# Router logits computed with the 36 logits as rows of PSUM, one table of places, expert weights computed later, and the first expert pair's tokens turned alone

## The chip, the cores and the metric

The kernel runs on one NeuronCore of one Trainium2 chip. The metric is the device time of one execution in microseconds (us). TensorE (PE in the profile, PEld for its weight loads) multiplies into PSUM; VectorE (DVE), ScalarE (ACT) and GpSimd (POOL) do the rest; SyncE (SP) issues the loads of weights, and POOL issues the DMAs that gather token rows. TensorE's clock is granted at one of two levels, 1.2 and 2.4 GHz; the profile prints it as 0.50 and 1.00.

## The reference

Two layers, 512 tokens of width 1024. Each layer is a mixer (attention and gated linear attention, left alone here) and a mixture of 32 experts in 4 groups of 8:

```python
for l in range(DEPTH):
    ...
    x = x + gate_m * hybrid_mixer(...)
    h = rms_norm(x, norm_ffn[l]) * (1.0 + scale_f) + shift_f
    x = x + gate_f * hierarchical_moe(h, ...)

def hierarchical_moe(h, ...):
    grp_prob = softmax(hf @ w_router_grp + b_router_grp)          # 4 groups
    grp_w, grp_idx = lax.top_k(grp_prob, 1)
    exp_logits = (hf @ w_router_exp + b_router_exp)               # 4 x 8 experts
    sel_logits = ...                                              # the 8 of the chosen group
    top_logit, top_idx = lax.top_k(sel_logits, 2)
    top_w = softmax(top_logit) * grp_w
    ...
    y = y + (silu(h @ w_gate) * (h @ w_up) * comb) @ w_down       # every expert, its tokens' weights
```

## The kernel before

A token goes through at most two experts. So the kernel computes the 36 logits of all tokens (4 groups, 32 experts), finds for each token its two experts and its place in each expert's list of up to 64 slots, gathers the token rows of each list from DRAM, and runs the experts two at a time ("pairs", 16 of them, each 128 slots).

**Router products** (`logits`, `logits_of`), still within the mixer. The residual `x` is turned on PE in blocks of 128x128 (tile `xT`), copied to SBUF by ACT and DVE in turn, and multiplied with the router's weights `wr`: the turned tokens are the stationary operand, 36 columns move, and the result `lg` has tokens as rows. Per layer these are 32 turns and 32 products. The last four blocks of columns are done token block by token block, as the output projection finishes them.

**From logits to lists** (`moe`). The tiles in order: `lo` (logits scaled by the token's inverse norm `rs`, plus `lc`), `first_max` three times (group, first and second expert), `eid`, `ex` (one-hot of the expert), `both`, the counting product `rk`, `pos` (place in the list), `ohp` (one-hot of the place, two tiles of 128x512), the product `nv` that carries token numbers into lists, `numbered` (numbers to indices `idx`, empty slots to a number out of bounds), and `fetch`, an indirect DMA on POOL for each pair. All this is one chain on DVE and PE. Beside it:

- ACT scales the tokens (`xn`, four instructions) and POOL writes them to DRAM (`xg`, four DMAs). A `fetch` reads `xg`.
- The routing weights (`ge`, `gs`, `gw`, `e2`, `den`, `cw`, `exw`) need two exponentials on ACT, which stand behind `xn` in ACT's queue. They are first used in `weights_by_slot`, after the first pair's first products.
- `keep_warm` puts products without use on PE, whose result (`warm`) nobody reads; each is 128x144.

**The first pair.** `gather(fetched[0:2])` turns the rows of pairs 0 and 1 together: 16 turns (tile `g`), then the scale and shift to `gT` by DVE and ACT, 128x256 each. `hidden` multiplies `gT` with the gate and up weights (tile `gu`), 16 instructions of 64 columns of the array each, two halves in turn. Then come `lst` and `slots` (from `weights_by_slot`), the turns for the next pairs, `d` (down product) and the next pair's `gu`.

The order on each engine comes from a scheduler; instructions wrapped in `keep_in_program_order` (`pm` among them) keep the program's order.

Of the kernel before, what the change touches and what calls it, by code (L numbers as in the profile page):

```python
# [20 lines left out]
P = 128  # L21
# [8 lines left out]
def hybrid_decoder_kernel(ctx, tc, x, c, w_ada, b_ada, norm_mix, norm_ffn, w_in, w_gk2, b_gk, q_gain,  # L30
# [132 lines left out]
    tok_i = ints[:, 407:407 + NT]  # L163
    G.iota(tok_i, pattern=[[P, NT]], base=1, channel_multiplier=1)
    tok = const.tile([P, NT], F, name="tok")
# [718 lines left out]

    def moe(l, xt, ss, pool):
# [31 lines left out]
        load_weights(9)  # L917
        wr, lc, lg = route.pop(l)
        rs = inv_rms(ss)
# [87 lines left out]
        def gather(fetched):  # L1007
# [4 lines left out]
            def make():  # L1012
                for k2 in range(KT // 2):
                    if k2 % 2 == 0:
                        gT.append(g4([P, 4, n], name="gT"))
                    ps = bank("g", "g", 2)
                    for k in (2 * k2, 2 * k2 + 1):
                        if k % 2:
                            yield
                        for j, r in enumerate(fetched):  # L1020
                            at = n * (k % 2) + P * j
                            tc.keep_in_program_order(T.transpose(ps[:, at:at + P], r[:, P * k:P * k + P], ident))  # L1022
                    for k in (2 * k2, 2 * k2 + 1):
                        src = ps[:, n * (k % 2):n * (k % 2) + n]
# [179 lines left out]

        ohp = [ohl([P, NT, 2, CAP], name="ohp") for _ in range(2)]
        for h in range(2):
            places_h = pos.rearrange("p t k -> p (t k)")[:, NT * h:NT * h + NT, None, None]
            tc.keep_in_program_order(V.tensor_tensor(ohp[h], iota[:, None, None, 0:CAP].to_broadcast([P, NT, 2, CAP]),
                                                     places_h.to_broadcast([P, NT, 2, CAP]), op=OP.is_equal))

        def by_slot(values, name):

            lst = misc(name, [P, NE])
            for i in range(NT * 2):
                pm(lst, ohp[i // NT][:, i % NT].rearrange("p a s -> p (a s)"), values[:, i], i == 0, i == NT * 2 - 1)
            return lst.rearrange("p (i a) -> p i a", a=2)

        idx = pool.tile([P, NE // 2], I32, name="idx")
        nv = by_slot(exn, "nv")
        for a in range(2):  # L1220
            numbered(nv[64 * a:64 * a + 64, :, a], idx[64 * a:64 * a + 64])
# [4 lines left out]
        gs = t3(1, "gs")
        A.activation(ge, ge, AF.Exp)
        V.reduce_sum(gs, ge, axis=AX.X)
        gw = t3(1, "gw")
        V.reciprocal(gw, gs)  # L1230
        cw = t3(2, "cw")
        e2 = t3(1, "e2")
        V.tensor_tensor(e2, m2, m1, op=OP.subtract)
        A.activation(e2, e2, AF.Exp)
        tc.keep_in_program_order(A.preload_act_table_set("silu_and_others"))
        den = t3(1, "den")
        V.tensor_scalar(den, e2, 1.0, None, op0=OP.add)
        V.reciprocal(den, den)
        V.tensor_tensor(cw[:, :, 0:1], den, gw, op=OP.mult)
        V.tensor_tensor(e2, e2, den, op=OP.mult)  # L1240
        V.tensor_tensor(cw[:, :, 1:2], e2, gw, op=OP.mult)
        dump(f"cw{l}", cw)
        exw = tmp.rearrange("p t k e -> p (t k) e")
        V.tensor_tensor(exw, ex.rearrange("p t k e -> p (t k) e"), cw.rearrange("p t k -> p (t k)")[:, :, None].to_broadcast([P, NT * 2, NE]), op=OP.mult)
# [147 lines left out]
```

## Time and profile before

| | |
|---|---|
| median of 3 runs | 1285.71 us (1284.75 to 1287.04) |
| profiled execution, its own time | 1283.96 us |
| its span in the trace | 1282.1 us |
| PE busy | 1172.3 us (91%) |
| DVE / ACT / POOL busy | 797.0 / 462.7 / 307.0 us |
| layer 0: router products, first `gu` | from 361.32, at 400.24 us |
| layer 1: router products, first `gu` | from 967.63, at 1003.37 us |

The profile shows one execution. In a row of the timeline the columns are start, duration, engine, line, operation, tiles (result <- operands), shape, count, and in brackets the idle time of the engine before it and what ended it. One fp32 product is two records on PE. Neighbouring records of a kind are merged, and the start of the next row tells when a merged one was over.

### The profile page before, as it was taken

To read this page: it belongs to the slowest core of one execution; us is meant where nothing else is said; L and a number is where in the kernel's file an instruction comes from. 1 tells how busy PE (TensorE), PEld (TensorE's weight loads), DVE (VectorE), ACT (ScalarE), POOL (GpSimd) and SP (SyncE) were. 2 spreads that over 40 slices of the span, in tenths; PEclk is the share of its full clock that TensorE was granted. 3 is DMA by queue.
4 is the path that set the end of the run, shared out by engine and by line. 5 is a ranking of instruction groups with operands and counts; after the bars stand their busy time and mean duration, and the time that the engine had idled before them with its cause. 6 is when DMAs were issued, how large, how long until landed. Compare 5 with 4: busy or idle time off the path is not lost. (4 is left out here: it accounts for less than half of the span.)

```text
span 1282.1 us, 16510 instructions
## 1 busy us (share of the span) xinstructions
PE 1172.3 (91%) x5935; PEld 739.7 (58%) x5935; DVE 797.0 (62%) x1484; ACT 462.7 (36%) x922; POOL 307.0 (24%) x330
## 2 busy tenths in 40 slices
PE   4989978977998999999988999899998899999996
PEld 2677746655885444444447877667787444444443
DVE  3488969796544555555546988877655355555553
ACT  3366635553251111111124775554535111111111
POOL 2122232244212222221103212434421222112110
PEclk9989989998979999999998999999998999999999
DMA  8454675751485999999805547763158699999961
GB/s 282 149 178 129 205 188 161 233 160 55 186 342 174 390 394 392 392 392 376 325 1 175 161 127 227 169 172 129 50 217 325 219 385 399 399 392 386 387 253 67
DMA packets 106285, 312.28 MB, mean 244 GB/s; under 512 B 13176, under 2 KB 50284, under 8 KB 81624
## 3 DMA queue, kind: packets, MB, share of 16 engines
q1 hardware_dynamic: 96920, 289.62, 62.6%
q0 software_dynamic: 9280, 21.57, 4.9%
q8 instruction: 48, 0.79, 0.3%
q14 instruction: 37, 0.30, 0.1%
HBM read 311.10 MB, written 8.43 MB: 249 GB/s over the span
## 5 line engine op out<-in xcount | busy, mean ns | idle before, releaser
L74 PE MATMUL proj<-whl,hh 128*128 128x512 f32 (+2 forms) x768 | 220.6, 370 | 7.4 <-ACT whl L95 6.2
L78 PE MATMUL gu<-wgu,gT 128*64 128x512 f32 x1024 | 225.8, 593 | 0.0
L1095 DVE TENSOR_TENSOR x<-y,x 128x512 f32<-128x512 f32 x240 | 153.9, 684 | 14.1 <-PE y L78 14.1
L78 PEld LDWEIGHTS gu<-wgu,gT 128*64 128x64 f32 x1024 | 73.5, 137 | 146.1 <-issue 146.1
L74 PEld LDWEIGHTS proj<-whl,hh 128*128 128x128 f32 x768 | 135.5, 191 | 36.1 <-issue 7.7
L1088 POOL TENSOR_TENSOR olo<-o,ohi 128x512 fp32r<-128x512 f32 x60 | 76.4, 1274 | 301.8 <-ACT ohi L1087 301.8
L96 POOL TENSOR_TENSOR whl<-raw,whl 128x512 fp32r<-128x512 f32 (+2 forms) x80 | 90.0, 1128 | 238.3 <-ACT whl L95 184.4
L1050 DVE TENSOR_TENSOR hs<-hs,gu 128x256 f32<-128x256 f32 x32 | 13.5, 421 | 204.4 <-ACT hs L1049 204.4
L74 PE MATMUL proj<-whl,hl 128*128 128x512 f32 (+2 forms) x384 | 139.0, 363 | 0.1
L255 DVE SCALAR_TENSOR_TENSOR row<-wada,ct,row 128x512 f32<-128x512 f32 x140 | 119.9, 856 | 16.8 <-DMA wada<-in_w_ada_dram 15.6
L78 PE MATMUL y<-ohi,oT 128*128 128x512 f32 x240 | 116.1, 484 | 6.9 <-DVE x L1095 6.9
L78 PE MATMUL d<-wd,hT 128*64 128x512 f32 x512 | 116.9, 598 | 1.4 <-ACT hT L1059 1.4
L1028 ACT ACTIVATE gT<-g,mod 128x256 f32<-128x256 f32 x64 | 35.9, 565 | 177.3 <-DVE gT L1030 177.3
L78 PE MATMUL y<-olo,oT 128*128 128x512 f32 x240 | 94.6, 394 | 0.0
L95 ACT ACTIVATE whl<-raw 128x512 fp32r<-128x512 f32 (+2 forms) x128 | 66.2, 524 | 68.3 <-PE proj L74 36.6
L78 PEld LDWEIGHTS y<-ohi,oT 128*128 128x128 f32 x240 | 44.8, 186 | 74.8 <-DVE x L1095 45.4
L74 PEld LDWEIGHTS proj<-whl,hl 128*128 128x128 f32 x384 | 72.6, 189 | 13.4 <-issue 3.0
L1049 ACT ACTIVATE hs<-gu 128x256 f32<-128x256 f32 x32 | 12.3, 384 | 169.9 <-PE gu L78 169.9
L78 PEld LDWEIGHTS d<-wd,hT 128*64 128x64 f32 x512 | 33.9, 136 | 62.2 <-issue 59.9
L1082 DVE SCALAR_TENSOR_TENSOR o<-d,cws,gate_f 128x512 f32<-128x512 f32 x64 | 47.7, 748 | 34.9 <-PE d L78 34.9
L1087 ACT ACTIVATE ohi<-o 128x512 fp32r<-128x512 f32 x60 | 37.8, 629 | 78.9 <-DVE o L1082 78.8
L1003 POOL DMA_INDIRECT rows<-xg,idx x32 | 32.8, 1025 | 126.0 <-PE g L1022 108.9
(339 smaller groups left out, 2041.6 us busy)
## 6 DMA issues: line engine op xcount, KB each, us to landing
wgu<-in_w_gate_dram SPq DMA_DIRECT2D x64, 1024.0 KB, 7.7
wgu<-in_w_up_dram SPq DMA_DIRECT2D x64, 1024.0 KB, 10.3
wd<-in_w_down_dram SPq DMA_DIRECT2D x64, 1024.0 KB, 8.8
wada<-in_w_ada_dram SPq DMA_DIRECT2D x96, 512.0 KB, 4.3
raw<-in_w_in_dram SPq DMA_DIRECT2D x80, 256.0 KB, 3.6
raw<-in_w_out_dram SPq DMA_DIRECT2D x16, 512.0 KB, 3.7
raw<-in_w_in_dram SPq DMA_DIRECT2D x32, 128.0 KB, 2.9
xg<-xn POOLq DMA_DIRECT2D x8, 512.0 KB, 2.9
```

The costliest lines, as they stand in the source:

```text
L74: T.matmul(o, a, b, start=start, stop=stop, skip_group_check=True)
L78: tc.keep_in_program_order(T.matmul(o, a, b, start=start, stop=stop, skip_group_check=True))
L95: A.activation(hi, src, AF.Copy)
L96: eng.tensor_tensor(lo, src, hi.bitcast(F), op=OP.subtract)
L255: V.scalar_tensor_tensor(row, ws[k], ct1[:, k:k + 1], row, op0=OP.mult, op1=OP.add)
L1003: G.indirect_dma_start(r, None, xg[:, :], bass.IndirectOffsetOnAxis(ap=idx, axis=0), bounds_check=S - 1, oob_is_err=False)
L1028: A.activation(o, src, AF.Identity, scale=m, bias=b)
L1050: V.tensor_tensor(hs[r], hs[r], gu[r, 256:512], op=OP.mult)
L1082: V.scalar_tensor_tensor(o, pd, cws[:, i:i + 1], gate, op0=OP.mult, op1=OP.mult)
L1087: A.activation(hi, o, AF.Copy)
L1088: (G if last is None else V).tensor_tensor(lo, o, hi.bitcast(F), op=OP.subtract)
L1095: V.tensor_tensor(xc, ps, xc, op=OP.add)
```

## The change

1. The logits' product is swapped round: `wr` is stationary, up to 512 tokens move, and the 36 logits are rows. Even blocks go to rows 0 to 35 of PSUM, odd ones to rows 64 to 99. Per token block both parts are copied to a zeroed tile `lgT` (DVE one, ACT the other), and a product with `two_parts` (two identities below each other) adds and turns them back into `lg`.
2. `lo` takes two instructions over all tokens instead of four.
3. Token numbers start from 1 - 65536, so `numbered` is one addition; `ohp` is one tile, and the lists have 64 rows for the even and 64 for the odd expert (16 products of 64x16 instead of 8 of 128x32).
4. The routing weights are issued only after `idx`.
5. Pair 0's rows are turned alone (a bank of PSUM then holds four turned blocks instead of two, each scaled in an instruction of 128x128); pair 1 is turned after pair 0's `gu`. All four fetches are still issued together. The second burst of `keep_warm` ahead of the turns has 20 products instead of 14.

```diff
@@ logits @@
-            lg = route[l][2] = misc("lg", [P, NT, 36])
+            lg = route[l][2] = [misc("lgT"), None]
...
-            for tt in range(NT):
-                mm(lg[:, tt], t[:, P * tt:P * tt + P], wr[:, k], tt == 0 and k == 0, k == KT - 1)
+            o = 64 * (k % 2)
+            mm(lg[0][o:o + 36], wr[:, k], t, k < 2, False)
@@ logits_of @@
+        c = slice(P * tt, P * tt + P)
         for k in range(4, KT):
-            mm(lg[:, tt], t[:, P * (k - 4):P * (k - 3)], wr[:, k], False, k == KT - 1)
+            o = 64 * (k % 2)
+            mm(lg[0][o:o + 36, c], wr[:, k], t[:, P * (k - 4):P * (k - 3)], False, k >= KT - 2)
+        t = s2([P, P], name="lgT")
+        G.memset(t, 0.0)
+        if lg[1] is None:
+            lg[1] = att("lg")[:, 0:NT * 36].rearrange("p (t e) -> p t e", t=NT)
+        for i, copy in enumerate((V.tensor_copy, A.copy)):
+            r = slice(64 * i, 64 * i + 36)
+            copy(t[r], lg[0][r, c])
+        mm(lg[1][:, tt], t, two_parts, tt == 0, True)
@@ moe @@
-        for tt in range(NT):
-            V.scalar_tensor_tensor(lo[:, tt], lg[:, tt], rs[:, tt:tt + 1], lc, op0=OP.mult, op1=OP.add)
+        V.tensor_tensor(lo, lg, rs[:, :, None].to_broadcast([P, NT, 36]), op=OP.mult)
+        V.tensor_tensor(lo, lo, lc[:, None, :].to_broadcast([P, NT, 36]), op=OP.add)
...
-            none = tiny.tile(list(idx.shape), F, name="none")
-            V.tensor_scalar(none, ps, 0.0, 65536.0, op0=OP.is_equal, op1=OP.mult)
-            V.scalar_tensor_tensor(idx, ps, -1.0, none, op0=OP.add, op1=OP.add)
+            return V.tensor_scalar(idx, ps, 65535.0, None, op0=OP.add)
...
-                for k2 in range(KT // 2):
+                nk = 512 // n
+                for k0 in range(0, KT, nk):
...
+                for a in range(2):
+                    pm(lst[64 * a:64 * a + 64], ohp[:, i], values[:, i, a::2], i == 0, i == NT * 2 - 1)
...
-        keep_warm(lo.rearrange("p t e -> p (t e)"), 14)
+        listed = numbered(by_slot(exn, "nv"), idx)
+        keep_warm(lo.rearrange("p t e -> p (t e)"), 20)
...
+        with tc.issue_after(listed.ins):
+            gs = t3(1, "gs")
+            A.activation(ge, ge, AF.Exp)
...
-        gT, rest = gather(fetched[0:2])
+        gT, rest = gather(fetched[0:1])
         for _ in rest:
             pass
+        gT1, second = gather(fetched[1:2])
...
-            *_, hs = hidden(now, P * (i % 2), [loaded.pop((0, e)) for e in (2 * i, 2 * i + 1)])
+            *_, hs = hidden(gT1 if i == 1 else now, 0 if i < 2 else P * (i % 2), [loaded.pop((0, e)) for e in (2 * i, 2 * i + 1)])
...
             if i == 0:
+                for _ in second:
+                    pass
                 weights_by_slot()
```

PE at the end of a mixer, layer 0, before (`op` is the output projection, `warm` a product of `keep_warm`):

```order
L74 MATMUL op<-wh,mixhl 128x512
L868 MATMUL xT<-ident,x 128x128 x12
L74 MATMUL lg<-wr,xT 128x36 x4
L868 MATMUL xT<-ident,x 128x128 x3
L74 MATMUL lg<-wr,xT 128x36 x8
L868 MATMUL xT<-ident,x 128x128
L879 MATMUL xT<-ident,x 128x128 x6
L74 MATMUL lg<-wr,xT 128x36 x4
L879 MATMUL xT<-ident,x 128x128 x3
L74 MATMUL lg<-wr,xT 128x36 x4
```

and the same place after the change, to the last product of the router:

```order
L872 MATMUL xT<-ident,x 128x128 x4
L74 MATMUL lgT<-xT,wr 36x512
L74 MATMUL lgT<-xT,wr 36x128 x4
L74 MATMUL lg<-two_parts,lgT 128x36
L883 MATMUL xT<-ident,x 128x128 x8
L74 MATMUL lgT<-xT,wr 36x128 x4
L883 MATMUL xT<-ident,x 128x128 x4
L74 MATMUL lg<-two_parts,lgT 128x36
L74 MATMUL lgT<-xT,wr 36x128 x4
L74 MATMUL lg<-two_parts,lgT 128x36
L74 MATMUL lgT<-xT,wr 36x128 x4
L74 MATMUL lg<-two_parts,lgT 128x36
```

Before, every product of a token block could be followed by turns; now each `lg` waits on PE for the two copies of the `lgT` product that stands right ahead of it, and the last two blocks have nothing between the two.

ACT at the end of the router products, after the change (before, the `lgT` copies were not there, and `xn` followed the last `xT` copy):

```order
L874 COPY xT<-xT 128x512
L896 COPY lgT<-lgT 36x128
L885 COPY xT<-xT 128x512
L896 COPY lgT<-lgT 36x128
L885 COPY xT<-xT 128x512
L896 COPY lgT<-lgT 36x128 x2
L937 ACTIVATE xn<-x,rs 128x1024 x4
```

`xn` now stands behind the last copy of the logits.

PE from the lists to the turns for the second pair of pairs, layer 0, before:

```order
L78 MATMUL warm<-lo,ident 128x144 x6
L78 MATMUL nv<-exn,ohp 128x32 x8
L78 MATMUL warm<-lo,ident 128x144 x14
L1022 MATMUL g<-ident,rows 128x128 x16
L78 MATMUL gu<-wgu,gT 64x512 x16
L78 MATMUL lst<-tmp,ohp 128x32 x8
```

and after the change:

```order
L78 MATMUL warm<-lo,ident 128x144 x6
L78 MATMUL nv<-exn,ohp 64x16 x16
L78 MATMUL warm<-lo,ident 128x144 x20
L1035 MATMUL g<-ident,rows 128x128 x8
L78 MATMUL gu<-wgu,gT 64x512 x16
L1035 MATMUL g<-ident,rows 128x128 x8
L78 MATMUL lst<-tmp,ohp 64x16 x16
```

Eight of the sixteen turns ahead of the first `gu` stand behind it now, ahead of `lst`.

## Rows read from the trace of the kernel before

**Rows 1.** Busy time of the engines in stretches of the span (stretch, length, then per engine the busy us and the number of instructions, granted clock of PE, busy share of the DMA engines, GB/s): layer 0's router products, layer 0's experts, layer 1's router products.

```profile
361.00:378.00 17.00, 16.48 (x99) 15.96 (x97) 4.44 (x13) 7.07 (x12) 0.58 (x1) 0.65 0.85 340
...
401.00:640.00 239.00, 235.88 (x1082) 103.80 (x1078) 124.34 (x222) 45.61 (x87) 47.16 (x40) 1.00 0.94 372
...
967.00:979.00 12.00, 11.75 (x100) 10.96 (x98) 4.29 (x12) 5.38 (x11) 0.00 (x0) 1.00 0.97 384
```

**Rows 2.** Timeline of PE, layer 0, from the first turn of the router to the first pair's products.

```profile
361.32 1.47 PE L868 MATMUL xT<-ident,x 128*128 128x128 f32 x12
...
374.08 3.47 PE L74 MATMUL lg<-wr,xT 128*128 128x36 f32 x16
378.45 5.01 PE L78 MATMUL warm<-lo,ident 128*128 128x144 f32 x20 [0.90 <-DVE xslot L1202]
...
388.67 3.68 PE L78 MATMUL warm<-lo,ident 128*128 128x144 f32 x28
394.69 0.33 PE L1022 MATMUL g<-ident,rows 128*128 128x128 f32 x1 [2.35 <-DMA rows<-xg,idx]
396.48 1.47 PE L1022 MATMUL g<-ident,rows 128*128 128x128 f32 x7 [1.46 <-DMA rows<-xg,idx]
...
400.24 7.09 PE L78 MATMUL gu<-wgu,gT 128*64 128x512 f32 x32
```

**Rows 3.** Timeline of PE, the same places of layer 1.

```profile
967.63 1.47 PE L868 MATMUL xT<-ident,x 128*128 128x128 f32 x12
...
976.87 1.98 PE L74 MATMUL lg<-wr,xT 128*128 128x36 f32 x16
...
990.48 2.00 PE L78 MATMUL nv<-exn,ohp 128*128 128x32 f32 x16
...
997.61 0.33 PE L1022 MATMUL g<-ident,rows 128*128 128x128 f32 x1 [1.61 <-DMA rows<-xg,idx]
...
1003.37 7.58 PE L78 MATMUL gu<-wgu,gT 128*64 128x512 f32 x32
```

**Rows 4.** Timeline of DVE between the logits and the fetches, layer 0 (first two rows) and layer 1.

```profile
383.38 0.17 DVE L1228 TENSOR_REDUCE gs<-gd 128x4 f32<-128x16 f32 x1 [0.90 <-ACT gd L1227]
...
389.28 0.38 DVE L998 SCALAR_TENSOR_TENSOR idx<-nv,none 64x16 int32<-64x16 f32 x2
...
986.04 0.17 DVE L1228 TENSOR_REDUCE gs<-gd 128x4 f32<-128x16 f32 x1 [2.27 <-ACT gd L1227]
...
989.41 0.68 DVE L1208 TENSOR_TENSOR ohp<-iota,pos 128x512 f32<-128x512 f32 x1
...
992.52 0.37 DVE L997 TENSOR_SCALAR none<-nv 64x16 f32<-64x16 f32 x2 [1.49 <-PE nv L78]
992.92 0.38 DVE L998 SCALAR_TENSOR_TENSOR idx<-nv,none 64x16 int32<-64x16 f32 x2
993.33 0.69 DVE L1256 TENSOR_TENSOR dg<-ident,slot 128x512 f32<-128x512 f32 x1
```

**Rows 5.** Timeline of ACT: the scaling of the tokens, layers 0 and 1.

```profile
374.86 8.39 ACT L923 ACTIVATE xn<-x,rs 128x1024 f32<-128x1024 f32 x4
...
977.61 8.30 ACT L923 ACTIVATE xn<-x,rs 128x1024 f32<-128x1024 f32 x4
```

**Rows 6.** Timeline of POOL, the last write of `xg` and the first fetches, layer 0 (first two rows) and layer 1; then the page's row of the writes (KB each, us from issue to landing) and the same of layer 1 alone.

```profile
383.54 0.53 POOL L88 DMA_DIRECT2D xg<-xn  x1 [1.55 <-ACT e L1234]
389.93 1.42 POOL L1003 DMA_INDIRECT rows<-xg,idx  x1 [5.86 <-DVE idx L998]
...
987.85 0.54 POOL L88 DMA_DIRECT2D xg<-xn  x1 [3.14 <-issue]
994.12 1.09 POOL L1003 DMA_INDIRECT rows<-xg,idx  x1 [5.72 <-DVE idx L998]
...
xg<-xn POOLq DMA_DIRECT2D x8, 512.0 KB, 2.9
...
xg<-xn POOLq DMA_DIRECT2D x4, 512.0 KB, 5.1
```

**Rows 7.** Stretches of 2 us, columns as in rows 1: granted clock of PE in layer 0 (first three) and layer 1.

```profile
364.00:366.00 2.00, 2.00 (x21) 2.00 (x20) 0.49 (x3) 0.24 (x2) 0.00 (x0) 1.00 1.02 422
366.00:368.00 2.00, 2.00 (x13) 2.00 (x11) 0.69 (x1) 0.59 (x1) 0.00 (x0) 0.53 1.01 422
...
382.00:384.00 2.00, 1.46 (x7) 1.24 (x6) 1.07 (x11) 1.98 (x4) 0.46 (x1) 0.71 0.65 262
...
980.00:982.00 2.00, 2.00 (x12) 2.00 (x12) 1.72 (x9) 2.00 (x2) 0.58 (x1) 0.63 0.98 410
```

**Rows 8.** Durations of the nearest operations: a pair's products and the first two products behind a pair's products (timeline of PE), a copy on ACT and two operations on DVE that read PSUM (groups by line: count, busy us, mean ns).

```profile
422.90 0.50 PE L78 MATMUL y<-ohi,oT 128*128 128x512 f32 x1
423.24 0.39 PE L78 MATMUL y<-olo,oT 128*128 128x512 f32 x1
...
432.67 7.04 PE L78 MATMUL gu<-wgu,gT 128*64 128x512 f32 x32
...
L1059 ACT COPY hT<-hsT 128x256 f32<-128x256 f32 x32 | 11.9, 373 | 19.6 <-PE hsT L1057 19.6
...
L683 DVE SCALAR_TENSOR_TENSOR st<-st,dec,kv 128x128 f32<-128x128 f32 x12 | 4.1, 340 | 0.8 <-PE kv L74 0.7
...
L484 DVE COPY lr<-proj 128x16 f32<-128x16 f32 x8 | 0.8, 157 | 0.0
```

More of the change, by code (lines that the diff above doesn't have):

```diff
@@ L131, in hybrid_decoder_kernel @@
     V.tensor_scalar(ident, jp, 0.0, None, op0=OP.is_equal)
+    two_parts = const.tile([P, 36], F, name="two_parts")
+    V.tensor_tensor(two_parts, ident[:, 0:36], ident[:, 64:100], op=OP.add)
     nU = const.tile([P, P], R, name="nU")
@@ L163, in hybrid_decoder_kernel @@
     tok_i = ints[:, 407:407 + NT]
-    G.iota(tok_i, pattern=[[P, NT]], base=1, channel_multiplier=1)
+    G.iota(tok_i, pattern=[[P, NT]], base=1 - 65536, channel_multiplier=1)
     tok = const.tile([P, NT], F, name="tok")
@@ L917, in moe @@
         load_weights(9)
-        wr, lc, lg = route.pop(l)
+        wr, lc, (_, lg) = route.pop(l)
         rs = inv_rms(ss)
@@ L1012, in make @@
             def make():
-                for k2 in range(KT // 2):
-                    if k2 % 2 == 0:
+                nk = 512 // n
+                for k0 in range(0, KT, nk):
+                    if k0 % 4 == 0:
                         gT.append(g4([P, 4, n], name="gT"))
                     ps = bank("g", "g", 2)
-                    for k in (2 * k2, 2 * k2 + 1):
+                    for k in range(k0, k0 + nk):
                         if k % 2:
@@ L1020, in make @@
                         for j, r in enumerate(fetched):
-                            at = n * (k % 2) + P * j
+                            at = n * (k - k0) + P * j
                             tc.keep_in_program_order(T.transpose(ps[:, at:at + P], r[:, P * k:P * k + P], ident))
-                    for k in (2 * k2, 2 * k2 + 1):
-                        src = ps[:, n * (k % 2):n * (k % 2) + n]
+                    for k in range(k0, k0 + nk):
+                        src = ps[:, n * (k - k0):n * (k - k0) + n]
                         m, b = mod[l][:, 4, k:k + 1], mod[l][:, 5, k:k + 1]
@@ L1202, in overflow_lists @@
             V.memset(xslot, 0.0)
[L1205 to L1209, printed above, removed]
+        ohp = ohl([P, NT * 2, CAP], name="ohp")
@@ L1211, in by_slot @@
+        tc.keep_in_program_order(V.tensor_tensor(ohp, iota[:, None, 0:CAP].to_broadcast([P, NT * 2, CAP]),
+                                                 pos.rearrange("p t k -> p (t k)")[:, :, None].to_broadcast([P, NT * 2, CAP]),
+                                                 op=OP.is_equal))
         def by_slot(values, name):
-            lst = misc(name, [P, NE])
+            lst = misc(name, [P, NE // 2])
             for i in range(NT * 2):
-                pm(lst, ohp[i // NT][:, i % NT].rearrange("p a s -> p (a s)"), values[:, i], i == 0, i == NT * 2 - 1)
@@ L1216, in by_slot @@
-            return lst.rearrange("p (i a) -> p i a", a=2)
+                for a in range(2):
+                    pm(lst[64 * a:64 * a + 64], ohp[:, i], values[:, i, a::2], i == 0, i == NT * 2 - 1)
+            return lst
         idx = pool.tile([P, NE // 2], I32, name="idx")
-        nv = by_slot(exn, "nv")
-        for a in range(2):
-            numbered(nv[64 * a:64 * a + 64, :, a], idx[64 * a:64 * a + 64])
-        keep_warm(lo.rearrange("p t e -> p (t e)"), 14)
+        listed = numbered(by_slot(exn, "nv"), idx)
@@ L1223, in moe @@
+        keep_warm(lo.rearrange("p t e -> p (t e)"), 20)
         fetched = [fetch(idx[:, i:i + 1]) for i in range(4)]
[L1226 to L1244, printed above, removed]
+        with tc.issue_after(listed.ins):
+            gs = t3(1, "gs")
+            A.activation(ge, ge, AF.Exp)
+            V.reduce_sum(gs, ge, axis=AX.X)
+            gw = t3(1, "gw")
+            V.reciprocal(gw, gs)
+            cw = t3(2, "cw")
+            e2 = t3(1, "e2")
+            V.tensor_tensor(e2, m2, m1, op=OP.subtract)
+            A.activation(e2, e2, AF.Exp)
+            tc.keep_in_program_order(A.preload_act_table_set("silu_and_others"))
+            den = t3(1, "den")
+            V.tensor_scalar(den, e2, 1.0, None, op0=OP.add)
+            V.reciprocal(den, den)
+            V.tensor_tensor(cw[:, :, 0:1], den, gw, op=OP.mult)
+            V.tensor_tensor(e2, e2, den, op=OP.mult)
+            V.tensor_tensor(cw[:, :, 1:2], e2, gw, op=OP.mult)
+            dump(f"cw{l}", cw)
+            exw = tmp.rearrange("p t k e -> p (t k) e")
+            V.tensor_tensor(exw, ex.rearrange("p t k e -> p (t k) e"), cw.rearrange("p t k -> p (t k)")[:, :, None].to_broadcast([P, NT * 2, NE]), op=OP.mult)
@@ L1250, in weights_by_slot @@
             lv = by_slot(exw, "lst")
-            V.tensor_copy(cws[0:64], lv[0:64, :, 0])
-            V.tensor_copy(cws[64:128], lv[64:128, :, 1])
+            V.tensor_copy(cws, lv)
             for k in range(2):
```

## The prediction

> **What bounds the kernel now.** I read the stretches first. In the experts' stage PE is busy 235.88 of 239 us at a granted clock of 1.00 [rows 1]: it runs as fast as PE does, so whenever its first `gu` starts earlier, the whole of the stage moves with it. The change touches only what lies between the first turn of the router and the first `gu`, twice. There the timeline of PE counts: from 361.32 to 400.24 us in layer 0 and from 967.63 to 1003.37 in layer 1 [rows 2, 3], 38.9 and 35.7 us. Everything is one chain, and I cut it where the last router product ends. Its records start at 374.08 and 976.87 and last 3.47 and 1.98, so this point (T) is 377.55 and 978.85. From the first turn to T it is 16.2 and 11.2 us, and from T to `gu` 22.7 and 24.5. The two layers differ before T by the clock alone: in layer 0 it fell from 1.00 to 0.53 at 366 [rows 7], amid the products of 36 columns; in layer 1 it was 1.00 throughout [rows 1].
>
> **The router products (T).** Before, 32 turns at 0.12 (1.47 for twelve, rows 2) are 3.9 us, and 32 products of 36 columns are the rest: 0.25 us each at the full clock (1.98 for eight, rows 3). After, per layer:
> - the 32 turns stay: 3.9 us.
> - 4 products of 512 columns. No row shows 36 of the array's columns; the nearest is `gu`, 64 columns, two halves in turn: 16 in 7.04 us [rows 8], 0.44 each. Where the other half is not there to run beside it, I bound it by twice that. Each waits for its own copy, so I take the middle of 1.8 and 3.5: 2.6 us.
> - 16 products of 128 columns: a quarter of 0.44 each, 1.75 us (3.5 alone; I take the former, since all four of a block are ready together).
> - 4 products into `lg`, 0.25 each: 1.0 us.
> - 4 round trips. PE stands and waits for `lgT`: a DVE copy, then the ACT copy, which is behind it by the zeroed tile that both write. No row has 36x128. DVE lies between 0.16 (16 columns) and 0.34 (128 columns, with arithmetic), ACT below 0.37 (256 columns) [rows 8]; I take 0.30 and 0.28 and 0.05 for each of three hand-overs: 0.73, four times 2.9 us.
>
> Sum 12.15 us at the full clock. That is 4.0 less than layer 0 took, and 0.9 more than layer 1: the swap saves PE's time, and the round trips give it back. The zeroing on POOL costs nothing: POOL was busy for 0.58 of these 17 us [rows 1]. The clock can go either way: the long products are like `gu`, which ran at 1.00 [rows 1], but the token blocks behind them leave PE waiting a third of the time. At the low level the 4.2 us of turns and products in the token blocks (12 turns, 16 and 4 products) double: 16.3. I take 13.5 for both layers, a third of the way from one end to the other, since the blocks hold only the second half. T moves by 16.2 - 13.5 = 2.7 earlier in layer 0 and by 2.3 later in layer 1. Both full: 4.0 and -0.9. Both low: -0.1 and -5.1.
>
> **From T to the indices.** `idx` ends at 389.66, T + 12.1, in layer 0 and at 993.30, T + 14.45, in layer 1 [rows 4]. Gone are: DVE's wait for ACT's `gd`, 0.90 and 2.27; `gs` itself, 0.17; two instructions of `none` and one of two for `idx` (from 992.52 to 993.30 it is 0.78, one instruction is 0.19): 0.6. In layer 1 `ohp` starts at 989.41, when its first half is done, but `nv` only at 990.48, held by a burst of `warm` at the low clock: 1.07, which goes when the burst starts earlier. So `idx` comes at T + 10.4 in layer 0 and T + 10.3 in layer 1. `nv` itself stays: twice as many products of half the columns of weights.
>
> **What is late next.** A fetch also needs the last write of `xg`, and that chain gets later. `xn` stood behind the last `xT` copy; it started 2.7 and 1.2 us before T. After the change it stands behind the last `lgT` copy, 0.3 before T (that copy, then one product of 0.25). It takes 8.35 [rows 5], POOL issues the last write 0.3 later (383.54 against 383.25) and it lands 2.9 after that [rows 6]: T + 11.25. So the write ends the wait, not `idx`, with 0.9 us between them; the first fetch starts 0.25 later as in layer 0 (389.66 to 389.93), at T + 11.5. In layer 1 the last write began late after `xn` (985.91 to 987.85 is 1.94, layer 0's 0.3 less is 1.65) and the landing of the four is 5.1 in the middle, beside the loads of weights; these loads end by then, and `xg` now comes later than they. I take layer 0's numbers for both.
>
> **From the fetch to `gu`.** PE waited from the first fetch's issue to its rows 4.8 us in layer 0 (389.93 to 394.69) and 3.5 in layer 1 (994.12 to 997.61) [rows 2, 3, 6]; I take 4.1: T + 15.6. The burst of 20 ahead of the turns starts with the end of `nv`, T + 10, and takes 5.3 at the full clock (3.68 for fourteen, rows 2): over at T + 15.3, just covered. Then 8 turns, 1.0, and the last scale's hand-over: `gu` at T + 16.65. For some turns at the low level (before, seven took 1.47 behind PE's idle time at 396.48, as long as twelve at 361.32, rows 2) I add 0.35: T + 17.0. What goes here is the wait for the second fetch and the eight turns behind it.
>
> **What comes back.** The eight turns of pair 1 stand behind the first `gu` now: 1.0 us per layer. Their scaling, four instructions each on DVE and ACT, is hidden by `lst` and `slots` on PE; without that cover it would be four times at most 0.34 [rows 8], 1.4. `weights_by_slot` still finds its weights long done. The other edits (`lo` in two instructions, `cws` in one, the table in the prelude) I cost at nothing: DVE's sum is the same to 0.2 us.
>
> **Sum.** Layer 0: 22.7 - 17.0 - 1.0 = 4.7, plus 2.7: 7.4. Layer 1: 24.5 - 17.0 - 1.0 = 6.5, less 2.3: 4.2. Together 11.6 us, from 1283.96 of the profiled execution to 1272.4. That execution lies 1.75 under the median of the runs, so I forecast 1285.71 - 11.6 = 1274.1.
>
> **Two rules weighed.** The first product of another kind behind `gu` starts 0.34 before the next one (422.90, 423.24) [rows 8] where 0.22 is usual (7.04 for 32): up to 0.12 more, and no idle time is shown between. The router part now has ten such changes per layer, between turns of the whole array and products of 36 columns: 1.2 us at most, which I keep for the range. The Trainium skill, page TensorEngine Tiling (Array Packing), Key Properties, says that a change of tiling mode drains TensorE; by that rule the ten cost this bound, and the gain would be 9.2 instead of 11.6. The row cannot tell the drain from any other change of operand.
>
> Beside the first fetch DVE ran `dg`, 993.33 to 994.02, and the fetch started at 994.12, 0.8 behind `idx` instead of 0.25; in layer 0 the fetch itself took 1.42, and 1.09 in layer 1 [rows 4, 6]. The Trainium skill, page SBUF — State Buffer, Who interferes with whom, infers that a tensor_tensor like `dg` does not keep GpSimd from writing descriptors, while 2-port modes of copy, cast and tensor_scalar do. The row speaks against the first half of it. By the rule the moved weights' instructions behind `idx` cost the fetch nothing; by the row up to 0.5 per layer. With the fetch a microsecond behind `idx` I take nothing.
>
> **Rivals.** (A) The forecast, gain 8 to 16 around 11.6. (B) `xg` is worse than I reckon: layer 1's late issue and slow landing (1.65 + 2.2) in both layers, 3.9 each. Gain 11.6 - 7.8 = 3.8, 1281.9. For it: nothing else ends the wait any more, and in layer 1 it was so. Against it: in layer 0 it was not, and the loads are over earlier than the writes now. (C) Clock full all through, and fetches as quick as layer 1's: T gives 3.1 over both layers instead of 0.4, and what follows is 0.6 + 0.35 shorter per layer. Gain 16.2, 1269.5. For it: PE streams more columns per product. Against it: PE has more holes. (D) Slower: the burst of 20. If the clock is low from the token blocks on and stays low, the burst takes 20 times 0.50 (5.01 for ten at the low level, rows 2), ten us from T + 11, and PE, which cannot pass it, lets the rows lie that are there at T + 16; turns at 0.21 follow, `gu` at T + 22.8. Layer 0: 22.7 - 22.8 - 1.0 - 0.1 = -1.2; layer 1: 24.5 - 22.8 - 1.0 - 5.1 = -4.4; 5.6 us slower, 1291.3. With T low in both layers 6.0 us of the gain are left, 3.0 per layer; a product at the low level is 0.24 longer, and 0.3 us are free ahead of the rows, so it decides from 14 of the 20 products. Against it: in layer 0 a burst of five us brought the clock back (low at 378.45, mixed from 382 to 384, full in the burst at 388.67, rows 2 and 7). (E) The change doesn't do what it says: the router part itself gets longer. That is half my forecast already (layer 1); alone, with nothing won behind it, it would be the both-low T, 5.2 slower, but the waits behind it are removed by program order, so I give this none.
>
> **How the numbers follow.** A 0.62, B 0.17, C 0.13, D 0.04, and 0.04 for small mishaps that end near no change. 0.2% is 2.6 us, what a measurement of this kernel tells from none. Faster than 1283.1 are A, C and nearly all of B: 0.92; the same 0.04; slower 0.04. The range reaches down to 1268, C and the 1.3 us by which the runs lie above their median, and up to 1281, where A with both clocks low (gain 6.0) loses another 1.2, half of the two layers' tiling price; what lies outside is D, the mishaps, and the worse half of B.
>
> **What would show it.** Right: from the first turn to the last `lg` 12 to 15 us in both layers; DVE passing from `bix` to `eid` without a wait; the first fetch ended by the write of `xg` (POOL's wait longer than `idx`); the rows at PE about 4 us later with `warm` just over; `gu` about 1.1 us behind the first `g`; eight `g` behind `gu`; the experts' stage as long as before plus 1 us. Wrong: a fetch that follows `idx` at once in both layers, idle PE of several us ahead of `g`, `warm` still running when the rows land, or an experts' stage that changed by more than 1 us.

## The result and the profile after

The changed kernel takes 1275.99 us (median of 15 runs, 1270.69 to 1283.80) against 1284.75 for the kernel before beside it: a ratio of 0.9933, 95% interval 0.9910 to 0.9956, so 8.6 us faster (5.7 to 11.6). Forecast: 11.6 us, 1274.1. The profiled run has a span of 1273.2 us, 8.9 less than before.

A span alone would mislead: between the last product of layer 0's experts and layer 1's router the same program took from 298.6 to 307.0 us in the profiles below (E2's, one of that kernel's longer runs, left out). What the change touches is therefore read from the first turn of a router to the second `gu` of its layer. Before, that is 54.62 and 51.92 us (361.32 to 415.94, 967.63 to 1019.55); after, 49.11 and 48.19: 9.24 us won. From the second `gu` to layer 0's last `y` it was 253.1 to 253.2 us in every profile.

Stretches, as in [rows 1]; the router parts are now 14 us long, at the full clock in both layers:

```profile
358.00:372.00 14.00, 10.86 (x81) 6.81 (x79) 5.30 (x15) 5.38 (x15) 0.82 (x4) 1.00 0.98 396
401.00:640.00 239.00, 235.30 (x1063) 103.17 (x1063) 130.22 (x231) 46.23 (x89) 45.77 (x38) 1.00 0.93 370
964.00:978.00 14.00, 10.98 (x82) 6.92 (x80) 5.21 (x14) 5.39 (x15) 0.82 (x4) 1.00 0.97 392
```

Timeline of PE, layer 0, against [rows 2]:

```profile
358.07 1.47 PE L872 MATMUL xT<-ident,x 128*128 128x128 f32 x12
359.61 1.91 PE L74 MATMUL lgT<-xT,wr 128*36 128x512 f32 x6
...
362.78 1.49 PE L74 MATMUL lgT<-xT,wr 128*36 128x512 f32 x10 [0.24 <-ACT xT L874]
365.00 0.41 PE L74 MATMUL lg<-two_parts,lgT 128*128 128x36 f32 x2 [0.74 <-ACT lgT L896]
...
366.56 0.63 PE L74 MATMUL lgT<-xT,wr 128*36 128x128 f32 x8 [0.24 <-ACT xT L885]
...
367.96 0.41 PE L74 MATMUL lg<-two_parts,lgT 128*128 128x36 f32 x2 [0.19 <-ACT lgT L896]
...
369.72 0.41 PE L74 MATMUL lg<-two_parts,lgT 128*128 128x36 f32 x2 [0.78 <-ACT lgT L896]
370.06 0.63 PE L74 MATMUL lgT<-xT,wr 128*36 128x128 f32 x8
371.47 0.41 PE L74 MATMUL lg<-two_parts,lgT 128*128 128x36 f32 x2 [0.78 <-ACT lgT L896]
...
380.01 1.11 PE L78 MATMUL nv<-exn,ohp 128*64 128x16 f32 x32 [0.37 <-DVE slot L1003]
381.05 5.17 PE L78 MATMUL warm<-lo,ident 128*128 128x144 f32 x40
388.28 1.09 PE L1035 MATMUL g<-ident,rows 128*128 128x128 f32 x8 [2.07 <-DMA rows<-xg,idx]
389.44 8.85 PE L78 MATMUL gu<-wgu,gT 128*64 128x512 f32 x32
398.23 1.09 PE L1035 MATMUL g<-ident,rows 128*128 128x128 f32 x8
399.25 1.11 PE L78 MATMUL lst<-tmp,ohp 128*64 128x16 f32 x32
```

and of layer 1, against [rows 3]:

```profile
977.59 0.41 PE L74 MATMUL lg<-two_parts,lgT 128*128 128x36 f32 x2 [0.77 <-ACT lgT L896]
...
984.09 3.19 PE L78 MATMUL warm<-lo,ident 128*128 128x144 f32 x12
987.21 1.11 PE L78 MATMUL nv<-exn,ohp 128*64 128x16 f32 x32
988.25 5.17 PE L78 MATMUL warm<-lo,ident 128*128 128x144 f32 x40
995.19 1.09 PE L1035 MATMUL g<-ident,rows 128*128 128x128 f32 x8 [1.77 <-DMA rows<-xg,idx]
996.35 7.16 PE L78 MATMUL gu<-wgu,gT 128*64 128x512 f32 x32
```

T, the end of the last router product, is 371.88 and 978.00, 13.8 us behind the first turn in both layers. `gu` follows at T + 17.6 and T + 18.35 (22.7 and 24.5 before), 1.16 us behind the first `g`. Layer 0's `gu` took 8.85 instead of 7.16 us, at a clock that was low in part (granted 0.50 from 390 to 392).

What ends the wait ahead of the fetch stands in the timelines of DVE, ACT and POOL:

```profile
376.69 0.16 DVE L980 SCALAR_TENSOR_TENSOR eid<-gix,bix 128x4 f32<-128x4 f32 x1
...
381.15 0.17 DVE L1010 TENSOR_SCALAR idx<-nv 128x16 int32<-128x16 f32 x1 [0.49 <-PE nv L78]
...
988.37 0.17 DVE L1010 TENSOR_SCALAR idx<-nv 128x16 int32<-128x16 f32 x1 [1.53 <-PE nv L78]
```

```profile
371.44 8.33 ACT L937 ACTIVATE xn<-x,rs 128x1024 f32<-128x1024 f32 x4
...
977.57 8.31 ACT L937 ACTIVATE xn<-x,rs 128x1024 f32<-128x1024 f32 x4
```

```profile
380.06 0.53 POOL L88 DMA_DIRECT2D xg<-xn  x1 [1.53 <-ACT gd L1239]
383.83 1.10 POOL L1015 DMA_INDIRECT rows<-xg,idx  x1 [3.24 <-DVE tmp L1256]
...
987.81 0.54 POOL L88 DMA_DIRECT2D xg<-xn  x1 [3.17 <-issue]
991.70 1.09 POOL L1015 DMA_INDIRECT rows<-xg,idx  x1 [3.34 <-DMA xg<-xn]
```

DVE passes `bix` to `eid` without a wait, and `idx` is done 2.5 and 3.2 us ahead of the fetch (T + 9.45 and T + 10.5). The fetch waits on DVE for `idx` only, not for the `tmp` that the first row names: its true releaser is the last write of `xg`, which it follows by 3.77 and 3.89 us (that write's packets are seen until 382.6 and 990.4, and E5 below shows the fetch following it again). ACT ends `xn` at 379.8 and 985.9; in layer 1 the fourth write leaves 1.9 us after that, as before [rows 6].

### The profile page after: what moved, and what is told of

It reads as the page before. It is cut to its first block, busy times and chain, and to the rows that moved or that the text cites. A ratio compares the mean times of both kernels' runs of the same rounds, so it can differ in the third digit from the quotient of the medians.

```text
span 1273.2 us, 16659 instructions
## 1 busy us (share of the span) xinstructions
PE 1164.5 (91%) x5991; PEld 726.4 (57%) x5991; DVE 802.3 (63%) x1487; ACT 467.9 (37%) x938; POOL 306.9 (24%) x338
## 5 line engine op out<-in xcount | busy, mean ns | idle before, releaser
L78 PEld LDWEIGHTS gu<-wgu,gT 128*64 128x64 f32 x1024 | 76.2, 138 | 144.7 <-issue 143.3
L1063 DVE TENSOR_TENSOR hs<-hs,gu 128x256 f32<-128x256 f32 x32 | 13.5, 421 | 204.9 <-ACT hs L1062 204.9
L258 DVE SCALAR_TENSOR_TENSOR row<-wada,ct,row 128x512 f32<-128x512 f32 x140 | 118.4, 846 | 18.3 <-DMA wada<-in_w_ada_dram 17.0
L1041 ACT ACTIVATE gT<-g,mod 128x256 f32<-128x256 f32 (+1 forms) x72 | 38.8, 542 | 163.3 <-DVE gT L1043 163.2
```

Source lines behind the costliest of these rows:

```text
L78: tc.keep_in_program_order(T.matmul(o, a, b, start=start, stop=stop, skip_group_check=True))
L258: V.scalar_tensor_tensor(row, ws[k], ct1[:, k:k + 1], row, op0=OP.mult, op1=OP.add)
L1063: V.tensor_tensor(hs[r], hs[r], gu[r, 256:512], op=OP.mult)
```

## The experiments

All profiles by stage, us (T as above; the last two columns are the median and the ratio to the kernel before beside it, with its 95% interval). Every stage column stands for one profile, so differences of a microsecond or two between rows mean little by themselves (the changed kernel and E12 are the same program).

| kernel | first turn to T, layers 0, 1 | T to `gu` | first turn to second `gu` | median | ratio |
|---|---|---|---|---|---|
| before | 16.2, 11.2 | 22.7, 24.5 | 54.6, 51.9 | 1284.75 | 1 |
| E8 before again | 11.2, 16.3 | 25.5, 22.1 | 53.6, 56.0 | 1282.48 (1 run) | |
| after | 13.8, 13.8 | 17.6, 18.4 | 49.1, 48.2 | 1275.99 | 0.9933 (0.9910 to 0.9956) |
| E12 after again | 14.0, 13.8 | 17.3, 19.2 | 47.3, 49.6 | 1267.17 (1 run) | |
| E1 lone turn | 16.3, 11.2 | 18.4, 20.3 | 51.5, 48.2 | 1273.41 | 0.9921 (0.9889 to 0.9953) |
| E4 both turned | 13.8, 14.0 | 22.1, 23.8 | 51.6, 53.9 | 1282.53 | 1.0001 (0.9975 to 1.0027) |
| E2 old products | 11.2, 11.2 | 18.3, 18.6 | 47.4, 46.2 | 1276.59 | 0.9920 (0.9888 to 0.9953) |
| E3 weights ahead | 14.0, 13.8 | 19.3, 19.5 | 49.8, 49.7 | 1278.34 | 0.9960 (0.9936 to 0.9983) |
| E9 two tables | 13.9, 13.8 | 17.3, 19.1 | 48.0, 50.4 | 1276.81 | 0.9948 (0.9919 to 0.9978) |
| E5 `xg` by ACT | 14.0, 13.8 | 31.1, 31.3 | 62.3, 63.5 | 1299.60 | 1.0126 (1.0100 to 1.0151) |
| E6 `xn` on GpSimd | 13.8, 13.8 | 15.7, 18.1 | 45.8, 50.0 | 1271.17 | 0.9918 (0.9886 to 0.9949) |
| E7 E2, E5, E6 in one | 11.2, 16.4 | 25.9, 26.2 | 55.4, 60.0 | 1293.68 | 1.0073 (1.0047 to 1.0100) |
| E10 E2 and E6 | 11.2, 11.2 | 18.2, 17.4 | 45.8, 45.1 | 1271.44 | 0.9918 (0.9888 to 0.9947) |
| E11 28 `warm` | 13.8, 13.8 | 17.6, 18.4 | 47.9, 48.6 | 1273.83 | 0.9932 (0.9903 to 0.9961) |

**E1, the lone turn alone** (the kernel before):

```diff
-        gT, rest = gather(fetched[0:2])
+        gT, rest = gather(fetched[0:1])
...
+        gT1, second = gather(fetched[1:2])
...
+                for _ in second:
+                    pass
```

> The kernel before with one part of the change alone: the first pair's rows are turned by themselves, the second pair's behind the first expert stage. Theory (most of the gain comes from here): before, the first turn stands 5.55 us (layer 0) and 5.76 us (layer 1) ahead of the first gu, after the change 1.16 us in both, so 4.4 and 4.6 go; eight turns of about 1.0 us in all come back behind the first gu in each layer: 7.0 us net, ratio 0.9945, and the stretch from the last router product to the first gu falls from 22.7 and 24.5 us to about 18.3 and 19.9. Rival (the gain comes from the router's products and the fuller clock behind them): at most 2 us, ratio 0.998 or more, because the rows of the first pair come no sooner.

Both layers win by what was expected (3.4 and 3.6), 3.15 and 3.68 us against the record of before; the ratio, 0.9921, lies lower than the expected 0.9945, which is inside its interval. Timeline of PE, layer 0:

```profile
389.44 1.10 PE L1023 MATMUL g<-ident,rows 128*128 128x128 f32 x8 [2.51 <-DMA rows<-xg,idx]
390.61 7.16 PE L78 MATMUL gu<-wgu,gT 128*64 128x512 f32 x32
397.70 1.09 PE L1023 MATMUL g<-ident,rows 128*128 128x128 f32 x8
398.62 1.87 PE L78 MATMUL lst<-tmp,ohp 128*128 128x32 f32 x16
```

**E4, the same part taken out of the changed kernel:**

```diff
-        gT, rest = gather(fetched[0:1])
+        gT, rest = gather(fetched[0:2])
...
```

> The changed kernel with both pairs' rows turned together ahead of the first gu, as before. It is the counterpart of the lone turn: theory 7.0 us worse than the changed kernel, ratio against before 0.9987, with 5.5 us again between the first turn and the first gu. Rival (router and clock carry the gain): no more than 2 us worse, 0.995 or less.

Its first pair in layer 1 waits twice again, and turns sixteen blocks (timeline of PE):

```profile
992.48 0.33 PE L1035 MATMUL g<-ident,rows 128*128 128x128 f32 x1 [3.38 <-DMA rows<-xg,idx]
994.37 1.76 PE L1035 MATMUL g<-ident,rows 128*128 128x128 f32 x7 [1.57 <-DMA rows<-xg,idx]
996.51 1.97 PE L1035 MATMUL g<-ident,rows 128*128 128x128 f32 x8 [0.38 <-ACT gT L1041]
```

With everything else changed, nothing measurable is left. The lone turn (with its four blocks to a bank) carries the gain: alone it is as fast as the whole change (0.9921 and 0.9933). By E4's interval the other parts together are worth at most 3.5 us either way. The stages agree, with one or two profiles of each kernel: from the first turn to the second `gu`, both layers together, the two records of before average 108.1 us, E1 takes 99.7, E4 105.5, and the two records of the changed kernel average 97.1. So the lone turn gives 8.3 or 8.4 us by either route, and the rest 2.6.

**E2, the products as before, and E8, the kernel before once more:**

```diff
-            mm(lg[0][o:o + 36], wr[:, k], t, k < 2, False)
+            for tt in range(NT):
+                mm(lg[:, tt], t[:, P * tt:P * tt + P], wr[:, k], tt == 0 and k == 0, k == KT - 1)
...
```

> The changed kernel with the router's products as before (36 columns, tokens as rows); all else stays changed. Theory (the fetch is bound by ACT's xn and the writes of xg, not by the router's last product): in layer 0 xn starts 13.4 to 13.5 us after the first turn of the router with either form, so nothing is lost there though the last product comes 2.4 us later; in layer 1 xn starts at 10.0 instead of 13.4 us and the first gu comes 2.6 to 3.4 us sooner; ratio against before 0.990 to 0.992, that is 2 to 3 us better than the changed kernel. Rival (the new form carries the gain, by its clock): the low clock comes back in layer 0's router and the stretch to the first gu; 2.4 us or more worse than the changed kernel, ratio 0.995 or more.

By stages E2 is 3.7 us better than the changed kernel, a little more than its theory had, and the low clock did not come back in either router. Over the whole time the two cannot be told apart.

> The kernel before once more, for one profile. Is the low clock in layer 0's router (0.50 from the sixth to the twenty-second microsecond after its first turn) a property of its 36-column products, or of the run? Theory of the prediction (of the products): again 16.2 us from the first turn to the last product, against 11.2 in layer 1. Rival (of the run): 11.2 in layer 0 too, as in the run with the old products in the changed kernel, whose clock was full there. The mixer, which is the same in both, differs by several us from run to run in either case.

E8's last sixteen records of products in layers 0 and 1, and DVE's wait in layer 0:

```profile
363.48 1.98 PE L74 MATMUL lg<-wr,xT 128*128 128x36 f32 x16
...
975.03 3.47 PE L74 MATMUL lg<-wr,xT 128*128 128x36 f32 x16
```

```profile
372.64 0.17 DVE L1228 TENSOR_REDUCE gs<-gd 128x4 f32<-128x16 f32 x1 [2.24 <-ACT gd L1227]
```

In E8 the layers have changed places against [rows 2, 3]. Over before, E8, E1, E2, E7 and E10 the old products fell to the low level in 4 of 12 routers and took 11.2 us in the other 8: 12.9 on the mean. The new ones took 13.8 to 14.0 in all 16; in five of these the clock fell too, but only at the last product, which cost 0.1 to 0.2 us. So the new form is steadier and, in this small sample, on the mean 1 us a layer longer, and it holds `xn` back as well (E2 and E10 have it sooner). And a quick router is partly eaten up in the kernel before: DVE's wait for `gd` was 0.90 in layer 0 with the slow router [rows 4] and is 2.24 with the quick one.

**E3, the weights not held back** (the block under `issue_after` is issued freely):

```diff
-        with tc.issue_after(listed.ins):
+        if listed is not None:
```

> The changed kernel with the routing weights no longer held behind the list of rows: gs and what hangs on it stand ahead of ex, both and exn again, and DVE waits there for the exp that ACT does behind its four xn. Theory: the exp ends 7.9 to 8.2 us after the last router product and DVE would reach gs at 4.9, so idx comes some 3 to 4 us later, at about T+13; the fetch goes at T+12.0 in layer 0 and T+13.7 in layer 1 now, so 1.3 us are lost in layer 0 and 0 to 0.5 in layer 1: ratio 0.9945. Rival one (the xg writes bound the fetch by so much that the order on DVE does not matter): no difference from the changed kernel, 0.9933. Rival two (DVE's multiplications just ahead of the fetch hold GpSimd's descriptors up): the fetch comes sooner against the end of the xg writes, and the kernel is 1 us or more faster, 0.9925 or less.

DVE and POOL in layer 0:

```profile
378.27 0.17 DVE L1240 TENSOR_REDUCE gs<-gd 128x4 f32<-128x16 f32 x1 [2.77 <-ACT gd L1239]
...
383.80 0.18 DVE L1010 TENSOR_SCALAR idx<-nv 128x16 int32<-128x16 f32 x1 [1.25 <-PE nv L78]
383.89 0.68 DVE L1267 TENSOR_TENSOR dg<-ident,slot 128x512 f32<-128x512 f32 x1
```

```profile
384.25 1.29 POOL L1015 DMA_INDIRECT rows<-xg,idx  x1 [5.29 <-DVE idx L1010]
```

Now `idx` binds, and T to the first `g` is 1.8 and 1.2 us longer than in the changed kernel: the theory, with both layers dearer than expected (1.3, and 0 to 0.5). **E9, the table in two halves, 128-wide lists, two steps for the numbers:**

```diff
-                for a in range(2):
-                    pm(lst[64 * a:64 * a + 64], ohp[:, i], values[:, i, a::2], i == 0, i == NT * 2 - 1)
+                pm(lst, ohp[i // NT][:, i % NT].rearrange("p a s -> p (a s)"), values[:, i], i == 0, i == NT * 2 - 1)
...
```

> The changed kernel with the table of places in two halves, 128-wide products for the lists and two steps a half for the numbers, as before. Theory: nv takes 1.94 instead of 1.11 us and idx comes four small operations instead of one, some 1.5 to 2 us later, which the writes of xg hide (idx stood 2.5 and 3.3 us ahead of the fetch); behind the first gu lst takes 1.97 instead of 1.04 us on TensorE, and nothing hides that: 1.0 us a layer, 2 us in all, ratio 0.9948. Rival (idx binds, the table is on the path): 2 to 3 us a layer, ratio 0.997 or more.

T to the first `g` stays (16.1 and 17.3 against 16.4 and 17.2): the fetch again follows the last write of `xg` by 3.76 and 3.93 us, and in layer 0 `idx`, at T + 11.0, comes 0.85 us ahead of it. Behind `gu`, `lst` is 1.87 instead of 1.11 us, so 0.8 a layer is what the one table gives there; the measured ratio agrees (0.9948 against 0.9933), but its interval does not exclude no difference.

**E5, the writes of `xg` from ACT's queue:**

```diff
-            kept_dma(G, xg[P * tt:P * tt + P, :], xn.rearrange("t k p -> t (k p)"))
+            kept_dma(A, xg[P * tt:P * tt + P, :], xn.rearrange("t k p -> t (k p)"))
```

> The changed kernel with the four writes of xg issued from ACT's own queue behind its xn, not from GpSimd. Theory (the writes of xg bound the first fetch; in layer 1 the fourth leaves GpSimd 1.9 us after its xn is done): idx stands ready 2.5 and 3.3 us ahead of the fetch, so with a landing time of 2.9 us as now layer 1's fetch comes 2.0 us sooner and layer 0's 0.2: ratio 0.9916. Rival (GpSimd is held up by DVE's multiplications behind idx, which end 0.5 and 1.1 us ahead of the fetch): no gain, and the fetch stands where it stood after them.

The expectation of a gain failed, for another reason than either theory's. Timeline of SP's queue and of POOL, layer 0:

```profile
341.81 0.43 SPq L923 DMA_DIRECT2D wgu<-in_w_gate_dram  x1
378.21 0.33 SPq L923 DMA_DIRECT2D wgu<-in_w_up_dram  x1
```

```profile
393.13 1.13 POOL L1015 DMA_INDIRECT rows<-xg,idx  x1 [23.58 <-DMA xg<-xn]
```

and what SP's queue waited for from 335 to 400 us (us in total, times, longest):

```profile
SPq L923 <- DMA xg<-xn: 39.7, 3, 36.0
```

The weight loads waited 36 us for a write of `xg`: in this program they and the writes from ACT's queue signal the same semaphores in turn, and a load waits until the write that had its semaphore has landed. That is a wait of the program and no price of the queue. Then the loads ran beside the last writes of `xg`; the writes took 10.2 us to land (the middle of the four) instead of 2.9. But `idx` was done at 382.47 there and DVE's last multiplication at 384.8, and the fetch went at 393.13, 0.88 us behind the landing of the last write: it does follow `xg`, and nothing on DVE. **E7** (E5's queue for three writes, E2, E6) failed the same way, with a wait of 31 us of the loads for `xg`:

> The changed kernel with the router's products as before, the fourth xn on GpSimd and the other three written from ACT's queue. Theory (either form of the products is as good until ACT's xn; the old one lets xn start at 10.0 us after the router's first turn instead of 13.4): xn done at 16.2, xg landed at 20.1, idx at T+9.4 to 10.4 = 20.6 to 21.6 us: the fetch at 20.8 and 21.8 us instead of 25.8 and 27.5, 5.0 and 5.7 us better than the changed kernel, ratio 0.985, if layer 0's router keeps the full clock. If its clock falls again to 1.2 GHz, as in the kernel before, T is 16.2 and nothing is won in layer 0: ratio 0.989. Rival (the new form of the products carries the gain): worse than the changed kernel.

**E6, the fourth `xn` on GpSimd:**

```diff
-        for tt in range(NT):
+        for tt in (3, 0, 1, 2):
...
+            if tt == 3:
+                G.tensor_scalar(xn, src, rs[:, tt:tt + 1], None, op0=OP.mult)
+            else:
+                A.activation(xn, src, AF.Copy, scale=rs[:, tt:tt + 1])
```

> The changed kernel with the fourth xn multiplied by GpSimd, ahead of ACT's three. Theory: ACT is done one xn of 2.08 us earlier, the last write of xg leaves 2.0 us sooner in both layers and the fetch follows it until idx binds (T+9.5): 2.0 us sooner in layer 0, 2.1 in layer 1; ratio 0.990. Loss to set against it: if GpSimd's multiplication slows DVE's copies beside it, up to 0.5 us a layer on the router's last product. Rival (idx or DVE's stream is what the fetch waits for): within 0.5 us of the changed kernel.

```profile
365.71 3.84 POOL L939 TENSOR_SCALAR xn<-x,rs 128x1024 f32<-128x1024 f32 x1
...
375.08 0.53 POOL L88 DMA_DIRECT2D xg<-xn  x1 [1.51 <-ACT gd L1243]
378.90 1.24 POOL L1019 DMA_INDIRECT rows<-xg,idx  x1 [3.29 <-DVE e L1249]
...
981.14 0.54 POOL L88 DMA_DIRECT2D xg<-xn  x1 [3.17 <-issue]
986.87 1.10 POOL L1019 DMA_INDIRECT rows<-xg,idx  x1 [5.19 <-DMA xg<-xn]
```

Layer 0's `gu` comes 1.9 us sooner and the router's products are not disturbed: the theory. Layer 1 gives 0.2 only. Its fourth write leaves 2.0 us sooner than in the changed kernel (T + 7.8 instead of T + 9.8), but takes 4.7 us to land instead of 2.9: between 983.8 and 985.4 three packets run one behind the other, one of 16 KB of instructions and two of 4 KB of that write. That the instructions held the write back is not shown. Over the whole time E6 cannot be told from the changed kernel. **E10, E6 with the products as before:**

> The changed kernel with the router's products as before and the fourth xn on GpSimd, all writes of xg from GpSimd. Theory (xg's last write binds the fetch; with the old products xn starts at 10.0 us after the router's first turn): the fetch at 20.8 us (layer 0) and about 22 us (layer 1, its fourth write 3.7 us behind the third) after the first turn, against 25.8 and 27.5 in the changed kernel, so 5 us better in each layer: ratio 0.986. Where the old products meet the low clock, 16.2 us to the last of them, that layer gains nothing; they did so in 3 of 8 routers recorded so far, in layer 0 or in layer 1 by the run, the new ones in none, so on the mean 0.989 or 0.990. Rival (the new products' steady clock is worth more than the start of xn): no better than the changed kernel with GpSimd's xn alone, 0.992.

The routers are won (11.2 twice), but T to `gu` hardly falls, and the fetch goes 22.8 and 23.7 us after the first turn where 20.8 and 22 were expected: `xn` now starts so early that its writes share the DMA engines with the weight loads until about 372, 18 us behind the first turn, and in layer 0 `nv` ran at the low clock and `idx` came at T + 10.8. By stages E10 is 6.4 us better than the changed kernel; the ratios, 0.9918 and 0.9933, overlap.

**E11, 28 products of `warm` instead of 20:**

> The changed kernel with 28 instead of 20 warming products ahead of the first pair's turn. The 20 end 14.3 us after the router's last product and the rows are there at 16.4 and 17.2, so TensorE stands idle 2.1 and 1.8 us, and in layer 0 the first gu then took 8.85 instead of 7.1 us at a clock that fell to 0.5. Theory: 8 more (2.07 us at full clock) fill the idle time, the clock holds, 1.8 us are won in layer 0 and 0 to 1 in layer 1, ratio 0.992 or less. Rival (the clock falls by something else than the idle time, or the products end behind the rows): no gain, or up to 0.3 us a layer lost.

Idle PE ahead of `g` shrinks to 0.17 and 0.90 us and both `gu` take 7.16. The whole is as the changed kernel (0.9932 and 0.9933), so the expected gain is not seen. **E12, the changed kernel once more:**

> The changed kernel once more, for one profile. Theory: from the router's first turn to its last product again 13.8 us in both layers (in all fourteen routers recorded with the new products it was 13.8 to 14.0, while the old ones took 11.2 eight times and 16.3 four times); the fetch follows the last packet of xg by 0.9 to 1.4 us; the low clock under layer 0's first gu, which cost 1.75 us, is of the run: that gu takes 7.1 to 7.2 us here or the cost lies in layer 1. From the first turn to the second gu 47 to 49 us in each layer. Rival: the low clock under layer 0's first gu is a lasting property of the changed kernel, 8.9 us again in layer 0 alone.

```profile
382.82 7.16 PE L78 MATMUL gu<-wgu,gT 128*64 128x512 f32 x32
...
987.92 7.77 PE L78 MATMUL gu<-wgu,gT 128*64 128x512 f32 x32
```

Layer 0's first `gu` ran at the full clock here, and layer 1's lost 0.6 us: the low clock under layer 0's first `gu` was of that run. That 28 products cure it is not shown, since with 20 it is absent in some layers too.

## Why the prediction was right, and where it was not

- **T.** Forecast 13.5, measured 13.8 in both: the number is right by luck, its parts are not. The clock stayed full, for whose fall 1.35 us had been added; in its place the parts took 1.65 us more than their sum of 12.15. By the starts of successive records in layer 0 the turns took 4.4 against 3.9, the twenty products into `lgT` 5.1 against 4.35, and the four into `lg` 1.35 against 1.0. The four round trips were nearly as sized (DVE's copy 0.28, ACT's 0.26; waits of 0.74, 0.19, 0.78 and 0.78, 2.5 against 2.9); two waits of 0.24 for an `xT` copy stood in no term.
- **The gain from T, 2.7 and -2.3.** Measured 2.4 and -2.6, but the step took layer 0's 16.2 and layer 1's 11.2 for properties of the layers. E8 shows them to be of the run. Against the mean of 12.9 the swap loses about 1 us a layer. One profile could not tell this.
- **From T to the fetch.** `xg` and not `idx` ends the wait, as forecast (E5, E9). Layer 0: T + 11.95 against 11.5. Layer 1: T + 13.7, because its fourth write again left 1.9 us late; "I take layer 0's numbers for both" is the step that failed, and rival B had the right mechanism for one layer with about half its price (the landing was quick, as forecast). Mis-sized was also the fetch's start behind its releaser: 0.25 was taken from `idx` in layer 0, but behind the last landing of `xg` it was 0.88 and 1.0 here. "`nv` itself stays" failed too: 1.11 instead of 1.94, hidden under `xg`.
- **From the fetch to `gu`.** Rows after 4.45 and 3.5 us (4.1 forecast), the burst over 2.1 and 1.8 us before them at the full clock (0.3 forecast), so rival D had no ground; `gu` 1.16 behind `g`. T + 17.0 was forecast, 17.6 and 18.35 came.
- **What comes back.** The eight turns cost 1.0, but `lst` gives 0.76 to 0.86 of it back (1.87 to 1.97 became 1.11), which the sum lacked. In layer 0 the low clock under `gu` took 1.7, not foreseen there.
- **Sum.** Layer 0: 5.5 (2.4 + 5.1 - 2.0) against 7.4; layer 1: 3.7 (-2.6 + 6.2 + 0.1) against 4.2. By the forecast's own steps, both layers together: fetch to `gu` less what comes back, which is the lone turn, 7.4 against 6.6; T to the fetch 2.0 against 4.7; T itself -0.2 against 0.4. So the lone turn was sized well, and the step from T to the fetch was counted at more than twice what it gave. The two records of each kernel give 97.1 against 108.1 us for both layers, 10.9; the times give 8.6 with 11.6 at the interval's edge. The measured time lies in the stated range, and A holds.
- **The weights behind `idx`.** Removing DVE's wait was counted with 0.9 and 2.27. In E3, which puts it back, `idx` comes 4.0 and 3.1 us later (T + 13.45 and T + 13.7); the write of `xg` hides all but 1.8 and 1.2 of it, from T to `g`.
- **The two rules.** Layer 0's 13.8 at the full clock is 1.65 above the sum of its parts, spread over turns and products that alternate. That is room enough for the 1.2 that changes of tiling were bounded by, and no run parts the two: the rule of the Trainium skill, page TensorEngine Tiling (Array Packing), Key Properties, stays neither shown nor refuted here. Beside `dg` the fetch in E3 started 0.28 us after `idx` in both layers and took 1.29 and 1.28 instead of 1.10: slowed by 0.2, not held. The Trainium skill, page SBUF — State Buffer, Who interferes with whom, is borne out on the start. The prediction's reading of its row, that `dg` may have made the 0.8 us of layer 1, is not borne out: in E5 the fetch started 0.88 us behind what it waited for although DVE had been idle for 8 us. Where the 0.2 comes from no run shows.

## What to carry to other kernels

Where a stage begins on a first block, turn that block alone and put the second behind the stage's first product: here that one part carried the gain. Look for the bound that takes over before paying for a shorter path to the old one: `idx` was made 2.5 and 3.2 us too early while a scaling and its write stood unshortened beside it. And take a second profile before explaining a difference between two stages of the same code.

## Not expected of the hardware

- The 36-column products met the low clock in one router of two, in layer 0 or in layer 1, in four of six profiles, and then ran at it for most of the router; the form with 512 and 128 columns met it in none of sixteen routers before the last product (in five at that one), with more idle PE in it. What decides it is open.
- Layer 1's fourth write of `xg` starts 3.66 to 3.72 us after the third in all twelve profiles in which GpSimd issues the four, with no wait of the program's but that for its `xn`; in layer 0 it starts 2.0 to 2.1 after. The cause is open; a 16-KB packet of instructions was seen beside it in some profiles and not in others.
- The lists' products with half the rows and half the columns, twice as many, took 1.06 to 1.11 us at the full clock where the whole ones took 1.87 to 1.97.
- GpSimd needed 3.84 us for a `tensor_scalar` of 128x1024 that takes ACT 2.08, and DVE's copies beside it kept their 0.28 us.
